# Batches of two block pairs in the attention stage of a two-layer hybrid encoder, with the PSUM banks divided anew

## The chip, the cores and the metric

The kernel runs on one core of a Trainium2 chip. The metric is the device time of one execution in microseconds (us). Times are medians of several executions; the profile is that of one more execution, with a time of its own.

## What is computed

A sequence of 2048 tokens with 1024 features passes two layers and a final norm. Layer 0 is a state-space scan and a convolution side by side. Layer 1 is attention over selected keys: a small indexer scores all admissible keys of a query, the 256 best are kept, and each of 16 query heads attends to them; four query heads share one key/value head. The part that the change touches, cut to what matters:

```python
def block(c):                      # 64 queries
    score = einsum("bqh,bqhs->bqs", wib, relu(einsum("bqhd,bsd->bqhs", qib, ki)))
    score = where(key_chunk <= c, score, -inf)
    _, idx = top_k(score, 256)
    logits = einsum("bqhgd,bqkhd->bqhgk", qb, k[idx]) * 64 ** -0.5
    p = softmax(where(valid, logits, -inf))
    return einsum("bqhgk,bqkhd->bqhgd", p, v[idx])
```

All of it is in float32. The kernel does not gather keys: it computes the scores of all admissible keys and adds a mask of 0 or -1e30.

## The kernel before

The program is traced in Python, and a scheduler then orders each engine's instructions by a model of their times, with earlier traced instructions first among those that are ready. An engine executes its list in order. `K.after(later, earlier)` adds an edge to that ordering between two instructions of one engine, without a semaphore.

Layer 0, the projections of layer 1 and the indexer come first, then the attention stage (class `Attend`), then the output projection (`layer1_out`). The attention stage goes through 16 row tiles of 128 queries, in the order `ORDER`; row tile i has nb = i+1 key blocks of 128 keys. Each row tile is done in two halves `kp` (two key/value heads, e = 0 and 1), each half in two units `hp`; a unit holds two query heads h for each e. So there are 64 units. Beside the attention, the selection of keys for row tiles 12 to 15 (`select_mask`, generator `beside`) runs on DVE, ACT and GpSimd; one step of it is traced for every `PACE` = 800 columns of scores.

For a unit, `weights` makes the scores: for each h and each half of up to 1024 keys, it takes two tiles of two PSUM banks (pool `pq`, one for each e), fills them by matmuls of at most 512 columns in two parts (high and low part of the keys, L1095), and reads each with one DVE instruction (L1099). This one scales, adds the mask, writes `lm` (tile `prob`) and keeps a running minimum `mx`, which the second half takes as its start value. One ACT instruction for each (h, e) then exponentiates the whole row (L1110).

`values` goes over groups (e, b): two key blocks of one e. Four transposes by TensorE (L1126: two blocks, two heads) fill one bank of pool `pt` (three banks, tag `pt`), ACT copies them to SBUF as `pT` (L1131; for more than 14 blocks every second group is copied by DVE, L1129), and two products with v (L1133) accumulate in the one bank of pool `pv`. A product fills 64 columns of the array; the two of a group write different halves of the partitions. Each product appears in the trace as two matmul records, each transpose as one. After the last group, ACT copies the sums (`ov`, L1137), TensorE transposes them (`ps_ot`, L1141) into the same bank, and DVE multiplies them by the gate and the inverse denominator (L1147, L1150).

The queries of the next half are transposed in `stacks` (`ps_q`, L772); these tiles also come from pool `pt`. In the main loop the scores of a unit are traced before the values of the unit before it:

```python
unit = (loaded[n], hp_, at.weights(loaded[n], hp_))
if hp_ == 0:
    ready(n + 1)
if pend:
    at.values(*pend)
pend = unit
```

`chunks(n)` already exists for the indexer: it cuts n columns into pieces of at most 512 within each 1024, and makes a piece 384 wide where 128 columns would be left over.

## Time and profile before

| | |
|---|---|
| median of 3 runs | 3005.96 us (3002.47 to 3012.47) |
| profiled execution | 3008.15 us |
| its span, first to last instruction | 3006.3 us |
| TensorE busy | 2754.0 us (92%) |
| DVE busy | 2127.9 us (71%) |
| ACT busy | 1694.8 us (56%) |
| GpSimd busy | 1118.3 us (37%) |
| mean granted TensorE clock | 0.969 |

Shares over the whole span are averages over stages. In a busy time, overlapping instructions of one engine count once; matmuls are pipelined, so TensorE can be busy all the time and still be slowed. What TensorE does is better read from the distances between the starts of its instructions in the timeline.

### The profile page before, as it was taken

What the parts mean: (1) busy time and instruction counts of PE and PEld (TensorE: products, weight loads), DVE (VectorE), ACT (ScalarE), POOL (GpSimd) and SP (SyncE); (2) the same over time, 40 slices, a digit from 0 to 9 for tenths busy, and PEclk for the clock granted to TensorE, in tenths of its full rate; (3) what the DMA queues carried; (4) which work ended last, traced back from release to release, by engine and by line L of the source; (5) the groups of instructions that cost most, each with busy time, mean ns of one, the idle gap of its engine ahead of it and who ended that gap; (6) DMA issues with size and microseconds to landing.
All of it is one profiled execution on the core that took longest, in us unless ns stands there. A gap on an engine that the chain in (4) does not pass through costs nothing.

```text
span 3006.3 us, 47629 instructions
## 1 busy us (share of the span) xinstructions
PE 2754.0 (92%) x17488; PEld 2223.8 (74%) x17488; DVE 2127.9 (71%) x4121; ACT 1694.8 (56%) x3202; POOL 1118.3 (37%) x1453
## 2 busy tenths in 40 slices
PE   7779998799999999899789898999989999999998
PEld 5657786677999898888778885666655666666787
DVE  8889895996354478979997877876777444456444
ACT  4122333334243688778856558888887767655311
POOL 3946132642231587765665323322322101001000
PEclk9889899899999999999899998999999999999999
DMA  3263554356557323223432424110110101001332
GB/s 135 72 131 127 161 158 81 114 168 194 183 186 249 100 71 109 77 84 104 140 109 77 128 92 162 38 57 29 61 38 28 49 18 43 22 5 50 123 126 98
DMA packets 233385, 300.40 MB, mean 100 GB/s; under 512 B 14144, under 2 KB 171072, under 8 KB 233024
## 3 DMA queue, kind: packets, MB, share of 16 engines
q1 hardware_dynamic: 233152, 297.37, 31.5%
q8 instruction: 137, 2.24, 0.3%
q14 instruction: 96, 0.79, 0.1%
HBM read 194.16 MB, written 105.25 MB: 100 GB/s over the span
## 4 chain that ended last, share of the span: by engine, by line
PE 41%; DVE 19%; issue 6%; ACT 5%; POOL 5%; DMA 3%; SPq 0%; DVEq 0%; ACTq 0%; POOLq 0%
PE ps_pv L1133 9%; PE ps_pt L1126 8%; PE ps_s L1095 7%; DVE eq L976 6%; PE ps_tm L121 2%; PE ps_tm L122 2%; PE ps_tm L123 2%; PE ps_o L122 2%; PE ps_o L121 2%; PE ps_o L123 2%; DVE scl L72 2%; POOL sv L69 2%; ACT eq L986 1%; DVE cum L1026 1%; POOL wl L114 1%
## 5 line engine op out<-in xcount | busy, mean ns | idle before, releaser
L114 POOL TENSOR_TENSOR wl<-wst,wh 128x512 fp32r<-128x512 f32 (+1 forms) x220 | 339.0, 1544 | 389.6 <-ACT wh L113 377.8
L121 PE MATMUL ps_tm<-wh,hb 128*128 128x256 f32 (+1 forms) x1536 | 439.4, 290 | 11.7 <-ACT ot L875 7.5
L122 PE MATMUL ps_tm<-wh,hb 128*128 128x256 f32 (+1 forms) x1536 | 444.1, 290 | 0.2 <-DVE hb L72 0.2
L123 PE MATMUL ps_tm<-wl,hb 128*128 128x256 f32 (+1 forms) x1536 | 438.8, 289 | 0.0
L1099 DVE CUSTOM_DVE_ANT_0 lm<-ps_s,amb 128x1024 f32<-128x1024 f32 (+7 forms) x256 | 250.3, 987 | 200.1 <-PE ps_pt L1126 117.2
L72 DVE SCALAR_TENSOR_TENSOR cvo<-hc,vec,cvo 128x1024 f32<-128x1024 f32 x240 | 359.3, 1529 | 0.8
L1131 ACT COPY pT<-ps_pt 128x512 f32<-128x512 f32 (+1 forms) x512 | 273.9, 564 | 152.3 <-PE ps_pt L1126 130.1
L1133 PE MATMUL ps_pv<-pT,v 128*64 128x256 f32 x2176 | 339.3, 398 | 14.4 <-DVE avt L62 7.5
L1126 PEld LDWEIGHTS ps_pt<-ident,lm 128*128 128x128 f32 x2176 | 240.1, 141 | 145.4 <-issue 124.5
L1126 PE MATMUL ps_pt<-ident,lm 128*128 128x128 f32 x2176 | 339.1, 282 | 6.1 <-ACT pT L1131 4.0
L1110 ACT ACTIVATE lm<-lm,mx 128x512 f32<-128x512 f32 (+15 forms) x256 | 309.1, 1211 | 62.9 <-DVE mx L1099 62.4
L69 POOL TENSOR_SCALAR sv<-sv 128x1 f32<-128x1 f32 x448 | 185.5, 415 | 382.6 <-DVE eq L976 296.5
L121 PEld LDWEIGHTS ps_tm<-wh,hb 128*128 128x128 f32 x1536 | 296.2, 194 | 21.2 <-ACT ot L875 9.2
L122 PEld LDWEIGHTS ps_tm<-wh,hb 128*128 128x128 f32 x1536 | 297.7, 194 | 6.0 <-DVE hb L72 0.6
L123 PEld LDWEIGHTS ps_tm<-wl,hb 128*128 128x128 f32 x1536 | 296.4, 194 | 4.8
L113 ACT CAST wh<-wst 128x512 fp32r<-128x512 f32 (+1 forms) x220 | 133.4, 610 | 277.2 <-DMA wst<-in_w_in 122.3
L1095 PE MATMUL ps_s<-kh,qs 128*128 128x512 f32 (+2 forms) x640 | 264.9, 415 | 19.4 <-DVE mx L1099 17.9
L121 PE MATMUL ps_p<-hh,wh 128*128 128x512 f32 x640 | 258.5, 406 | 19.1 <-ACT uT L520 16.0
L123 PE MATMUL ps_p<-hl,wh 128*128 128x512 f32 x640 | 258.9, 407 | 0.0
L122 PE MATMUL ps_p<-hh,wl 128*128 128x512 f32 x640 | 257.5, 403 | 0.0
L1095 PE MATMUL ps_s<-kl,qs 128*128 128x512 f32 (+2 forms) x640 | 233.4, 370 | 0.0
L913 ACT ACTIVATE relu<-ps_i 128x512 f32<-128x512 f32 (+3 forms) x304 | 161.0, 545 | 104.5 <-DVE scl L72 55.3
(327 smaller groups left out, 6353.0 us busy)
## 6 DMA issues: line engine op xcount, KB each, us to landing
wst<-in_w_in SPq DMA_DIRECT2D x168, 256.0 KB, 2.9
zs_d<-zt SPq DMA_DIRECT2D x16, 512.0 KB, 3.5
zt<-zs_d SPq DMA_DIRECT2D x16, 512.0 KB, 4.5
ry<-rec_d SPq DMA_DIRECT2D x16, 512.0 KB, 4.2
xr<-in_x SPq DMA_DIRECT2D x16, 512.0 KB, 4.3
wst<-in_w_out SPq DMA_DIRECT2D x32, 256.0 KB, 3.3
h_d<-xr SPq DMA_DIRECT2D x16, 512.0 KB, 3.5
xt<-h_d SPq DMA_DIRECT2D x16, 512.0 KB, 6.1
```

The source lines that it names most:

```text
L69: eng.tensor_scalar(out=out, in0=a, scalar1=s1, scalar2=s2, op0=op0, op1=op1)
L72: self.nc.vector.scalar_tensor_tensor(out=out, in0=a, scalar=s, in1=b, op0=op0, op1=op1)
L114: nc.gpsimd.tensor_tensor(out=lo, in0=st, in1=hi.bitcast(F32), op=ALU.subtract)
L121: t.matmul(ps, a[0], b[0], start=start, stop=False)
L122: t.matmul(ps, a[1], b[0], start=False, stop=False)
L123: t.matmul(ps, a[0], b[1], start=False, stop=stop)
L1095: nc.tensor.matmul(pss[e][:, cols], qs[e][:, 2 * hp + h], src[:, e, cols], start=part == 0, stop=part == 1)
L1099: self.pace[0] = nc.vector.tensor_tensor_reduce(out=prob[e][h][:, c:c + w], in0=pss[e][:, 0:w], in1=mb[:, c:c + w], scale=-0.125, scalar=( ...
L1110: nc.scalar.activation(lm, lm, AF.Exp, bias=mxs[e, h][:, nh - 1:nh], scale=-1.0, accum_out=t["den"][:, hd:hd + 1])
L1126: nc.tensor.transpose(ps[:, s, h], prob[e][h][:, (b + s) * P:(b + s + 1) * P], ident)
L1131: nc.scalar.copy(pT[:, 0:n], ps[:, 0:n].rearrange("p s h q -> p s (h q)"))
L1133: nc.tensor.matmul(po[64 * s:64 * s + 64, e], self.kvt[(b + s) // 8, kp][2][:, (b + s) % 8, e * 64:e * 64 + 64], pT[:, s], start=b == 0, s ...
```

## The change

1. `weights`: the scores of each h go over `chunks(nk)`, pieces of at most 512 columns. For each piece two one-bank tiles are taken (pool `pq`, now three banks in place of two tiles of two), filled by four matmuls and read by one DVE instruction each. The running minimum passes from piece to piece; `mx` has five columns.
2. `values`: groups are handled in batches of `TURN` = 2. `turned` makes the transposes and the copy of one group, `weighted` the products of a batch. The products of a batch are traced after the transposes of the next batch, and an edge ties the first of them behind the last of these transposes. Another edge (`held`) ties the first transpose of a call behind the last product of the call before.
3. Pool `pt2` has four banks in place of three. Eight PSUM banks are in use before and after.

```diff
--- before.py
+++ after.py
@@ -1041,7 +1041,7 @@
         self.k, self.S, self.kvt, self.ident, self.identr = k, S, kvt, ident, identr
         self.am, self.tm, self.qsp, self.ap, self.pp, self.ptp, self.pq, self.pt, self.pv_ = pools
         self.beside, self.pace, self.cols = beside, pace, 0
-        self.masks = {}
+        self.masks, self.held = {}, None
 
     def load(self, i, kp):
 
@@ -1072,7 +1072,7 @@
 
         k, nc, ap_, kvt = self.k, self.k.nc, self.ap, self.kvt
         nk = (t["i"] + 1) * P
-        kp, qs, mb, nh = t["kp"], t["qs"], t["mb"], (nk + HALF - 1) // HALF
+        kp, qs, mb, ch = t["kp"], t["qs"], t["mb"], chunks(nk)
         prob = [[None, None], [None, None]]
         mxs = {}
         for h in range(2):
@@ -1082,24 +1082,21 @@
                 elif h == 0:
                     both = self.pp[e].tile([P, 2, HALF], F32, tag="lm", name="lm")
                     prob[e] = [both[:, 0], both[:, 1]]
-                mxs[e, h] = ap_.tile([P, 2], F32, tag="mx", name="mx", bufs=8)
-            for half in range(nh):
-                c = half * HALF
-                w = min(HALF, nk - c)
-                kh, kl, _ = kvt[half, kp]
-                pss = [self.pq.tile([P, HALF], F32, tag="pq", name="ps_s") for _ in range(2)]
-                for b in range(0, w, 512):
-                    cols = slice(b, b + max(min(512, w - b), 256))
-                    for part, src in enumerate((kh, kl)):
-                        for e in range(2):
-                            nc.tensor.matmul(pss[e][:, cols], qs[e][:, 2 * hp + h], src[:, e, cols],
-                                             start=part == 0, stop=part == 1)
+                mxs[e, h] = ap_.tile([P, 5], F32, tag="mx", name="mx", bufs=8)
+            for ci, (c, w) in enumerate(ch):
+                pss = [self.pq.tile([P, 512], F32, tag="pq", name="ps_s") for _ in range(2)]
+                half, m = c // HALF, max(w, 256)
+                cols = slice(c % HALF, c % HALF + m)
+                for part in range(2):
+                    for e in range(2):
+                        nc.tensor.matmul(pss[e][:, 0:m], qs[e][:, 2 * hp + h], kvt[half, kp][part][:, e, cols],
+                                         start=part == 0, stop=part == 1)
                 for e in range(2):
                     mx = mxs[e, h]
                     self.pace[0] = nc.vector.tensor_tensor_reduce(
                         out=prob[e][h][:, c:c + w], in0=pss[e][:, 0:w], in1=mb[:, c:c + w], scale=-0.125,
-                        scalar=(-NEG if half == 0 else mx[:, 0:1]), op0=ALU.add, op1=ALU.min,
-                        accum_out=mx[:, half:half + 1])
+                        scalar=(-NEG if ci == 0 else mx[:, ci - 1:ci]), op0=ALU.add, op1=ALU.min,
+                        accum_out=mx[:, ci:ci + 1])
                     self.cols += 2 * w
                     while self.cols >= PACE:
                         self.cols -= PACE
@@ -1107,7 +1104,7 @@
             for e in range(2):
                 lm = prob[e][h][:, 0:nk]
                 hd = 4 * e + 2 * hp + h
-                nc.scalar.activation(lm, lm, AF.Exp, bias=mxs[e, h][:, nh - 1:nh], scale=-1.0,
+                nc.scalar.activation(lm, lm, AF.Exp, bias=mxs[e, h][:, len(ch) - 1:len(ch)], scale=-1.0,
                                      accum_out=t["den"][:, hd:hd + 1])
         return prob
 
@@ -1117,22 +1114,46 @@
         nb, kp = t["i"] + 1, t["kp"]
         np_ = P if nb > 1 else 64
         po = self.pv_.tile([P, 2, 256], F32, tag="pv", name="ps_pv")
-        for e in range(2):
-            for b in range(0, nb, 2):
-                n = min(2, nb - b)
-                ps = self.pt.tile([P, 2, 2, 128], F32, tag="pt", name="ps_pt")
+
+        def turned(group):
+
+            e, b = group
+            n = min(2, nb - b)
+            ps = self.pt.tile([P, 2, 2, 128], F32, tag="pt", name="ps_pt")
+            for s in range(n):
+                for h in range(2):
+                    op = nc.tensor.transpose(ps[:, s, h], prob[e][h][:, (b + s) * P:(b + s + 1) * P], ident)
+                    if self.held is not None:
+                        k.after(op, self.held)
+                        self.held = None
+            pT = self.ptp.tile([P, 2, 256], F32, tag="pT", name="pT")
+            if b % 4 == 2 and nb > 14:
+                nc.vector.tensor_copy(pT[:, 0:n], ps[:, 0:n].rearrange("p s h q -> p s (h q)"))
+            else:
+                nc.scalar.copy(pT[:, 0:n], ps[:, 0:n].rearrange("p s h q -> p s (h q)"))
+            return e, b, n, pT, op
+
+        def weighted(groups, last):
+
+            for e, b, n, pT, _ in groups:
                 for s in range(n):
-                    for h in range(2):
-                        nc.tensor.transpose(ps[:, s, h], prob[e][h][:, (b + s) * P:(b + s + 1) * P], ident)
-                pT = self.ptp.tile([P, 2, 256], F32, tag="pT", name="pT")
-                if b % 4 == 2 and nb > 14:
-                    nc.vector.tensor_copy(pT[:, 0:n], ps[:, 0:n].rearrange("p s h q -> p s (h q)"))
-                else:
-                    nc.scalar.copy(pT[:, 0:n], ps[:, 0:n].rearrange("p s h q -> p s (h q)"))
-                for s in range(n):
-                    nc.tensor.matmul(po[64 * s:64 * s + 64, e],
-                                     self.kvt[(b + s) // 8, kp][2][:, (b + s) % 8, e * 64:e * 64 + 64], pT[:, s],
-                                     start=b == 0, stop=b + s >= nb - 2)
+                    op = nc.tensor.matmul(
+                        po[64 * s:64 * s + 64, e],
+                        self.kvt[(b + s) // 8, kp][2][:, (b + s) % 8, e * 64:e * 64 + 64], pT[:, s],
+                        start=b == 0, stop=b + s >= nb - 2)
+                    if last is not None:
+                        k.after(op, last)
+                        last = None
+            self.held = op
+
+        groups = [(e, b) for e in range(2) for b in range(0, nb, 2)]
+        before = None
+        for g in range(0, len(groups), TURN):
+            now = [turned(group) for group in groups[g:g + TURN]]
+            if before:
+                weighted(before, now[-1][4])
+            before = now
+        weighted(before, None)
         ov = ap_.tile([P, 2, 256], F32, tag="ov", name="ov", bufs=2)
         nc.scalar.copy(ov[0:np_], po[0:np_])
         ps = self.pv_.tile([P, 2, 2, 128], F32, tag="pv", name="ps_ot")
@@ -1156,6 +1177,7 @@
 ORDER = (3, 7, 4, 6, 5, 8, 2, 9, 1, 10, 11, 12, 0, 13, 14, 15)
 RATIO = 2
 CHAINS = 3
+TURN = 2
 EARLY = 140
 PACE = 800
 LATE = 12
@@ -1275,8 +1297,8 @@
             am, tm = pool(c3, "am", 1, side="right"), pool(c3, "tm", 1, side="right")
             ptp, ap_ = pool(c3, "ptp", 4, side="right"), pool(c3, "ap", 1, side="right")
             pp1, qsp = pool(c3, "pp1", 3, side="right"), pool(c3, "qsp", 1, side="right")
-            pools = (am, tm, qsp, ap_, (pp0, pp1), ptp, pool(c3, "pq", 2, space=PSUM),
-                     pool(c3, "pt2", 3, space=PSUM), pool(c3, "pv", 1, space=PSUM))
+            pools = (am, tm, qsp, ap_, (pp0, pp1), ptp, pool(c3, "pq", 3, space=PSUM),
+                     pool(c3, "pt2", 4, space=PSUM), pool(c3, "pv", 1, space=PSUM))
             at = Attend(k, S, kvt, pools, ident, identr, beside, pace)
             halves = [(i, kp) for i in ORDER for kp in range(2)]
             loaded = {}
```

## Rows read from the trace of the kernel before

**Rows 1.** Busy times by stretch: from:to, length, each engine (instructions), clock, DMA

```profile
1815.00:2310.00 495.00, 455.92 (x2946) 308.92 (x2945) 369.29 (x799) 422.88 (x771) 136.20 (x255) 0.98 0.16 53
2310.00:2809.00 499.00, 496.47 (x3232) 325.52 (x3230) 255.28 (x502) 312.62 (x494) 65.31 (x90) 1.00 0.10 32
```

**Rows 2.** Waits of weight loads, 1815 to 2310 us: total us, times, longest

```profile
PEld ps_pt L1126 <- issue: 49.8, 129, 0.8
PEld ps_s L1095 <- DVE mx L1099: 29.5, 42, 2.5
...
PEld ps_pv L1133 <- ACT pT L1131: 13.6, 35, 2.2
```

**Rows 3.** The same view, 2310 to 2809 us

```profile
PEld ps_pt L1126 <- issue: 74.7, 194, 0.4
```

**Rows 4.** Timeline of TensorE, groups one by one: start us, length us, instruction, count

```profile
2403.84 0.66 PE L1126 MATMUL ps_pt<-ident,lm 128*128 128x128 f32 x4
2404.42 0.65 PE L1133 MATMUL ps_pv<-pT,v 128*64 128x256 f32 x4
2405.01 0.66 PE L1126 MATMUL ps_pt<-ident,lm 128*128 128x128 f32 x4
```

**Rows 5.** Timeline of TensorE, a place where two groups went together

```profile
2649.72 1.09 PE L1126 MATMUL ps_pt<-ident,lm 128*128 128x128 f32 x8
2650.74 1.08 PE L1133 MATMUL ps_pv<-pT,v 128*64 128x256 f32 x8
2651.75 0.66 PE L1126 MATMUL ps_pt<-ident,lm 128*128 128x128 f32 x4
```

**Rows 6.** Timeline of TensorE, first and last run of value products

```profile
1827.42 0.65 PE L1133 MATMUL ps_pv<-pT,v 128*64 128x256 f32 x4
...
2806.97 1.52 PE L1133 MATMUL ps_pv<-pT,v 128*64 128x256 f32 x12
```

**Rows 7.** Timeline of TensorE, query transposes between value products

```profile
2308.40 0.65 PE L1133 MATMUL ps_pv<-pT,v 128*64 128x256 f32 x4
2308.98 0.53 PE L772 MATMUL ps_q<-identr,tmq 128*128 128x128 f32 x4
2309.45 0.65 PE L1133 MATMUL ps_pv<-pT,v 128*64 128x256 f32 x4
```

**Rows 8.** Timeline of TensorE, scores between transposes and value products

```profile
2406.18 0.66 PE L1126 MATMUL ps_pt<-ident,lm 128*128 128x128 f32 x4
2406.59 0.48 PE L1095 MATMUL ps_s<-kh,qs 128*128 128x512 f32 x1
...
2407.47 0.65 PE L1133 MATMUL ps_pv<-pT,v 128*64 128x256 f32 x4
```

**Rows 9.** Timeline of TensorE, score pieces of 384 and 512 columns

```profile
2639.88 0.34 PE L1095 MATMUL ps_s<-kl,qs 128*128 128x384 f32 x1
2640.05 0.39 PE L1095 MATMUL ps_s<-kh,qs 128*128 128x512 f32 x1
2640.28 0.40 PE L1095 MATMUL ps_s<-kl,qs 128*128 128x512 f32 x1
```

**Rows 10.** DVE by line and shape, 1815 to 2810 us: busy us, mean ns, idle before

```profile
L1099 DVE CUSTOM_DVE_ANT_0 lm<-ps_s,amb 128x1024 f32<-128x1024 f32 x144 | 175.5, 1221 | 149.3 <-PE ps_pt L1126 92.1 <-PE ps_s L1095 56.6
...
L1099 DVE DVE_READ_ACCUMULATOR2_ANT mx<- 128x1 f32 x384 | 31.9, 83 | 0.0
...
L1099 DVE CUSTOM_DVE_ANT_0 lm<-ps_s,amb,mx 128x512 f32<-128x512 f32 x16 | 11.9, 749 | 11.1 <-PE ps_s L1095 11.0
...
L1099 DVE CUSTOM_DVE_ANT_0 lm<-ps_s,amb 128x512 f32<-128x512 f32 x16 | 10.7, 688 | 3.4 <-PE ps_s L1095 3.2
```

**Rows 11.** By stretch, instructions that write or read `lm`: PE, PEld, DVE, ACT

```profile
1815.00:2310.00 495.00, 154.99 (x996) 110.88 (x996) 169.34 (x207) 168.84 (x318) 0.98 0.16 53
```

**Rows 12.** ACT by line, 1815 to 2810 us: busy us, mean ns, idle before

```profile
L1110 ACT ACTIVATE lm<-lm,mx 128x512 f32<-128x512 f32 (+15 forms) x256 | 309.1, 1211 | 62.9 <-DVE mx L1099 62.4
L1131 ACT COPY pT<-ps_pt 128x512 f32<-128x512 f32 (+1 forms) x512 | 273.9, 564 | 152.3 <-PE ps_pt L1126 130.1 <-PE ps_pv L1133 20.8
```

## The prediction

> **What bounds the kernel now.** I read the table of time stretches first. The change touches only the attention stage, which runs from about 1815 to 2809 us of a span of 3006.3 us; I cut it at 2310 us, shortly before the selection of keys that runs beside it ends. In the second part TensorE is busy for 496 of 499 us, and DVE for only 255 and ACT for 313 [rows 1]. In the first part TensorE is busy for 456 of 495 us, ACT for 423 and DVE for 369 [rows 1]: three engines are close to each other there, and TensorE waits for them. So a saving on TensorE shortens the second part in full and the first part only partly. What follows the stage starts when its rows are done, so I pass a shorter stage on to the end in full.
>
> Next the waits. In the first part TensorE's weight loads stand still 29.5 us for a minimum from DVE (a score bank not yet read) and 13.6 us for ACT's copy of transposed weights [rows 2]. In both parts the largest entry has no releaser at all: before a transpose that follows a value product, 129 and 194 times, some 0.39 us each [rows 2, 3]. The timeline shows what that is. Call T the four transposes of one group (two key blocks) and W its two value products (four records). Where T and W alternate, T at 2403.84, W at 2404.42, T at 2405.01, one round takes 1.17 us [rows 4]. Where two groups went together, T8 at 2649.72, W8 at 2650.74, T4 at 2651.75, two groups took 2.03 us [rows 5]. Two rounds would be 2.34 us, so each round saved is worth 0.31 us: TensorE pays at each turn between the full-width transposes and the products that fill half of its columns.
>
> Counted along the timeline, from the first value product at 1827.42 to the last at 2806.97 [rows 6], the 576 groups are executed in 406 unbroken runs of value products: 175 for 242 groups in the first part, 231 for 302 in the second (the rest lies at the cut and in records missing from the trace). Turns thus cost about 406 x 0.31 = 126 of the 994 us.
>
> **The change part by part.** *Fewer turns.* Every call of `values` has an even number of groups, so two make a batch: 288 batches. The edges written out give T T, then W of the batch before, and the next call's transposes come after the last W, so the last two batches of a call share one run. With nothing else in between, a call of n batches has n-1 runs (one if n=1). That is 104 runs in the first part and 127 in the second.
>
> Two things break runs. Queries' transposes use the same banks as T and cut runs now: W at 2308.40, query transposes at 2308.98, W at 2309.45 [rows 7]; only these stand between two runs in 20 places of the first part and 15 of the second. I keep all of them. Scores are traced before the values and enter wherever a bank falls free. Between T and W they cost no further turn (T at 2406.18, scores at 2406.59, W at 2407.47 [rows 8]), between two W they do. Now that is 13 and 9 places. A batch of four products offers three inner places instead of one, and a score bank frees once per 512 columns, not per 1024, so up to twice as often. Threefold would be 39 and 27, sixfold 78 and 54. I take 25 and 35, since in the second part the batches are longer; the first part's share is near its old value because its runs are shorter. Runs afterwards: 104+20+25 = 149 and 127+15+35 = 177. Saved: 26 and 54, together 80 x 0.31 = -24.8 us. The ends are none (0 us) and all (406-231 = 175 runs, -54 us).
>
> *Score pieces.* For 5 and 13 key blocks the old cut leaves 512 and 256 columns computed, the new one 384 and 256. A piece of 512 takes 0.23 us (2640.05 to 2640.28), one of 384 takes 0.17 (2639.88 to 2640.05) [rows 9]. 32 matmuls in each of the two row tiles save 0.06: -3.8 us. The rest of the score columns stays.
>
> *More reduces on DVE.* Pieces go from 24 to 40 over the 16 row tiles, times 16: 384 reduces become 640. Splitting 1024 columns replaces 1221+83 ns by 688+83 and 749+83 ns [rows 10]: 299 ns each, 256 x 0.299 = 76.5 us of DVE. 112 of them, 33.5 us, belong to the ten row tiles of the first part, 43 us to the second. In the second part the cover is DVE's idle 244 us, so I cost it at nothing there. In the first, DVE would be busy 403 of 495 us. TensorE waits 29.5 us there for 169 us of reduces [rows 11], 0.17 us per us; at that rate 33.5 us more cost +6 us. Ends: 0, and 33.5 if DVE passes everything on. Two things speak for the lower half: the third bank lets the next piece of one head begin before the other's is read, and a 0.7 us reduce blocks DVE's queue for less time than a 1.2 us one. Behind each reduce on DVE are queued the next piece's reduce, the selection's counts and, for 15 and 16 key blocks, half of the weights' copies.
>
> The Trainium skill has a rule that speaks against this part (VectorE: DVE Perf Modes, on the trn2 errata): a fixed cost per DVE instruction, measured there as about 150 cycles at 0.96 GHz, so that many small pieces pay it each. Worked out from that page it is an estimate of 256 x 0.156 = 40 us, 17.5 of it early. The rows show 299 ns for a split and not 156, because the second piece takes its start value from a column and each piece has an accumulator read of its own [rows 10]; I use 299.
>
> *A longer way from T to W.* W now follows the next batch's T, so a copy by ACT (564 ns on average [rows 12]) has a T8 and the W8 before it, 2.03 us, to finish, against one round of 1.17. That takes away part of the first part's 13.6 us: -7, between -13.6 and 0. Four T banks hold two batches, and four `pT` buffers do too, since W of a batch is issued before the T that needs its buffers again.
>
> *The ends of the calls.* The last W has only the W of the batch before to cover its copies, 1.0 us for two copies in sequence, and the next call's transposes may not come first. ACT is in an exponential for 309 of 994 us, 1.2 us at a time [rows 12]. If one is in the way (one call in three) W waits about 0.8 us unless scores fill it: 64/3 x 0.8 = 17 us at most; the 8 calls of one batch have no cover, about 1.2 us each or 10 us. Scores of the next unit stand before values in priority and should fill most. I take +6, between 0 and 27; nearer to 0, as calls now end T, W with one group's cover and the second part shows hardly a wait.
>
> Sum: -24.8 -3.8 +6 -7 +6 = -23.6 us. The profiled execution took 3008.15 us (span 3006.3); 3008.15-23.6 = 2984.5. It lies 2.2 us above the median of 3005.96, so the forecast for the median is 2982.
>
> **The rivals.** *Scores cut the batches up.* Every bank that falls free starts its own pair of score matmuls, up to 640 entries. If 80 more than I took fall inside a run of W, the turns stay at 406. Left are -3.8+6-7+6 = +1: 3007, no change. For it: entries get shorter and more frequent. Against: of some 300 entries now only 22 stand alone between two runs.
>
> *The first part becomes DVE's* (the slower side). All 33.5 us of the additional reduces reach TensorE through the score banks, the relief of 7 us disappears in it, and the call ends cost 6: -24.8-3.8+33.5+6 = +11, 3017. It becomes slower than can be told from no change (0.3%, 9 us) when additional waits exceed 24.8+3.8+9 = 37.6 us. For it: DVE at 369 of 495 us and 29.5 us of waits on it already; against: ACT is busier there, and DVE also waits for TensorE's scores.
>
> *Clean batches.* No score and no query cuts a run (231 runs, -54), pieces -3.8, all 13.6 us of the copies' waits go and nothing is added: -71, 2935; with the query cuts left and half of the waits, -54+11-3.8-7 = -54, 2952.
>
> *The edges don't hold.* Each binds one instruction only. If the others pass it, the order remains near the old one, with the pieces and the reduces changed: about -3.8+6, 3008.
>
> **How the numbers follow.** Forecast 0.47 (2970 to 2997), cut-up batches 0.20, DVE 0.14, clean batches 0.14, edges 0.05. Faster by over 0.3%: nearly all of the first, the clean batches and a little of the cut-up ones, 0.62; within 0.3%: 0.22; slower: the DVE case and a tail of the others, 0.16. The range goes from the moderate clean case, 2950, to the DVE case, 3017; beyond lie half of the clean and half of the DVE chance.
>
> **What would show it.** Runs of value products near 326, most of eight records, and fewer than 323 entries "transpose, no releaser". In the second part of the stage TensorE still without waits and some 18 us shorter. 640 reduces at about 690 to 750 ns. In the first part, the wait of scores for DVE: under 40 us for the forecast, over 60 for the DVE rival. The wait of value products for ACT's copy: less than 13.6 us in the first part; if it grows, the call ends were priced too low. I am wrong in the main step if runs stay near 400, and wrong in the sum if runs fall and a wait on DVE or ACT takes their place.

## The result, and the profile after

| | before | after |
|---|---|---|
| median, beside each other | 3004.22 us (4 executions) | 3034.28 us (4; 3023.94 to 3041.96) |
| ratio, 95% interval | 1 | 1.0092 [1.0065, 1.0118] |
| profiled execution | 3008.15 us | 3023.94 us |
| its span | 3006.3 us | 3022.2 us |
| attention stage, first score to last value product | 1814.6 to 2808.1 | 1808.2 to 2819.8 |
| first part, to the end of the tenth row tile | 518.6 us | 548.5 us |
| second part | 475.5 us | 463.6 us |
| unbroken runs of value products, by part | 184 + 222 | 171 + 192 |
| mean granted TensorE clock | 0.969 | 0.966 |

The kernel became slower by about 0.9%, where 0.8% faster was forecast. A second measurement of the same kernel gave 1.0084 [1.007, 1.0098] (e14 below). The four executions of the first took 3023.94, 3030.53, 3038.03 and 3041.96 us at mean clocks of 0.966, 0.964, 0.962 and 0.960, and the profile is of the fastest; it shows half of the loss in the medians. The stretch ahead of the stage was 6.4 us shorter in it. That stretch has the same order of TensorE's instructions in both kernels, so I take its 6.4 us as scatter from execution to execution. The stage grew by 18.1 us, all in the first part. In the profile of e14, the same kernel at about its median (3031.05 us), the stage is 23.6 us longer than before. One execution of e1 below ran in a slower state of the chip (3113.51 us at a clock of 0.837); its median counts it, its ratio doesn't. From here on the parts are cut at the end of the tenth row tile, not at 2310 us, so that both kernels have the same work in them.

Busy times of the kernel after, by stretch (columns as in [rows 1]; PE, PEld, DVE, ACT, POOL, clock, DMA):

```profile
1808.00:2357.00 549.00, 490.98 (x3097) 330.96 (x3098) 410.81 (x1068) 439.90 (x802) 138.20 (x262) 0.95 0.15 53
2357.00:2820.00 463.00, 458.88 (x3057) 303.61 (x3055) 251.60 (x744) 292.12 (x464) 59.32 (x84) 1.00 0.09 29
```

TensorE fills the second part as before. In the first part it stands for 58 us, against 40 before with the same cut, and its clock is 0.95, against 0.98 in [rows 1].

Waits of weight loads in the kernel after, first part, then second (line, releaser, total us, times, longest):

```profile
PEld ps_s L1092 <- DVE mx L1096: 56.2, 70, 5.0
PEld ps_pt L1125 <- issue: 39.2, 96, 0.8
PEld ps_pv L1140 <- issue: 37.5, 105, 2.8
PEld ps_pv L1140 <- ACT pT L1133: 11.5, 30, 2.3
```

```profile
PEld ps_pt L1125 <- issue: 48.9, 127, 0.4
PEld ps_pv L1140 <- ACT pT L1133: 15.8, 47, 1.3
```

Against [rows 2], the wait of scores for DVE has nearly doubled, from 29.5 us (31.2 with the parts cut as here) to 56.2, and its longest has gone from 2.5 to 5.0 us. The entry "transpose, no releaser" fell as forecast, from 129 and 194 to 96 and 127 times. Beside it stands "value product, no releaser". It was there before too, 73 and 156 times, in lines that [rows 2] and [rows 3] leave out (1815 to 2310 us, then 2310 to 2809):

```profile
PEld ps_pv L1133 <- issue: 17.4, 73, 1.5
```

```profile
PEld ps_pv L1133 <- issue: 30.6, 156, 0.4
```

After, these are 105 times and 37.5 us in the first part, 96 times and 23.1 us in the second. So in the first part some of what was saved before transposes is paid again before products.

Here is one of the long waits, in the timeline of DVE and TensorE (some other instructions left out):

```profile
2248.97 2.35 DVE L976 TENSOR_SCALAR_CACHE_REDUCE eq<-khi,sv 128x2048 bf16<-128x2048 uint16 x1
...
2249.32 0.33 PE L1092 MATMUL ps_s<-kl,qs 128*128 128x384 f32 x1
...
2251.24 2.35 DVE L72 SCALAR_TENSOR_TENSOR klo<-khi,sv,klo 128x2048 uint16<-128x2048 uint16 x1
...
2253.57 0.68 DVE L1096 CUSTOM_DVE_ANT_0 lm<-ps_s,amb 128x512 f32<-128x512 f32 x1
...
2254.31 0.69 PE L1092 MATMUL ps_s<-kh,qs 128*128 128x384 f32 x1 [4.66 <-DVE mx L1096]
```

The scores of a piece are in their bank at about 2249, but two instructions of the selection (a count, L976, and an update of `klo`, L72) are ahead of the reduce in DVE's queue. The next score matmul needs that bank and stands 4.66 us at the head of TensorE's queue; all that is behind it, transposes and products too, stands with it. During the waits of scores in the first part such selection instructions ran on DVE for 4.3 us before and for 25.5 us after.

What follows the wait costs again. Busy times around it, and TensorE's timeline there:

```profile
2243.00:2249.00 6.00, 5.84 (x40) 4.13 (x40) 5.83 (x17) 4.79 (x8) 1.90 (x5) 1.00 0.12 44
2249.00:2254.00 5.00, 0.66 (x5) 0.34 (x3) 5.00 (x5) 0.91 (x2) 1.99 (x4) 1.00 0.18 52
2254.00:2259.00 5.00, 4.69 (x19) 3.11 (x20) 3.31 (x15) 3.92 (x6) 1.29 (x2) 0.50 0.19 60
```

```profile
2255.25 1.98 PE L1140 MATMUL ps_pv<-pT,v 128*64 128x256 f32 x8
2257.16 1.97 PE L1125 MATMUL ps_pt<-ident,lm 128*128 128x128 f32 x8
```

TensorE was busy for 0.66 of 5 us, and in the next 5 us its granted clock is 0.50, the lower level of 1.2 GHz. Eight products take 1.98 us and eight transposes 1.97, against 1.08 and 1.09 in [rows 5]. In the first part, distances within runs of products or transposes that are about double occur 8 times before and 70 times after; what they cost beyond the single distance is 1.4 and 11.2 us.

**The account.** I took every distance between two starts on TensorE in the stage, subtracted the steady distance of that kind of matmul, and counted a rest over 150 ns as a wait and a shorter one as turn. Doubled distances of products and transposes are taken out of both and stand by themselves; score matmuls at the lower clock are left among the waits and turns.

| after minus before, profiled executions | us |
|---|---|
| stretch ahead of the stage | -6.4 |
| waits | +25.4 |
| products and transposes at the lower clock | +9.8 |
| turns | -9.5 |
| score pieces of 384 columns | -3.8 |
| rest of TensorE's work, mainly the output projection not yet begun in the stage | -3.9 |
| last value product to the end | +4.2 |
| sum (span: +15.9) | +15.8 |

The turns themselves did what was forecast: the rests from product to transpose and from transpose to product fell from 55.9 to 34.8 us. The scores gave it back in short rests, 31.1 to 41.5 us between score matmuls, 13.4 to 22.2 from a score to a product and 3.5 to 9.3 from a product to a score. All other rests together fell by 13.4 us, about half of that between two transposes.

The last two lines above the sum belong together: they are work that moved. Before, the output projection's first matmul comes 18 us ahead of the last run of value products, and 24 of its matmuls (some 5.5 us) lie inside the stage; after, it begins behind the last product:

```profile
2788.94 0.48 PE L121 MATMUL ps_o<-wo,yh 128*128 128x512 f32 x1
```

```profile
2818.21 1.95 PE L1140 MATMUL ps_pv<-pT,v 128*64 128x256 f32 x16
2820.08 0.50 PE L121 MATMUL ps_o<-wo,yh 128*128 128x512 f32 x1
```

The first fence is of the kernel before (its last run of products is in [rows 6]), the second of the one after. TensorE is full in both cases, so little is lost or gained by it. Of the 12 us by which the second part is shorter, some 5 are therefore no gain.

**One statement ahead of this is wrong.** The section on the change, and the prediction with it, say that the `held` edge ties a call's first transpose behind the last product of the call before. In the code every `weighted` sets `self.held`, within a call too. So the first transpose of every further batch is tied behind the last product before it, and together with the other edge this gives a strict alternation: transposes of a batch, products of the batch before, transposes of the next. The order may not place transposes ahead of a product that will wait.

### The profile page after: what moved, and what is told of

It reads as the page before. It is cut to its first block, busy times and chain, and to the rows that moved or that the text cites. A ratio compares the mean times of both kernels' runs of the same rounds, so it can differ in the third digit from the quotient of the medians.

```text
span 3022.2 us, 48310 instructions
## 1 busy us (share of the span) xinstructions
PE 2751.4 (91%) x17488; PEld 2223.9 (74%) x17488; DVE 2167.6 (72%) x4633; ACT 1691.0 (56%) x3202; POOL 1110.3 (37%) x1453
## 4 chain that ended last, share of the span: by engine, by line
PE 42%; DVE 18%; issue 6%; POOL 5%; ACT 4%; DMA 3%; SPq 0%; DVEq 0%; ACTq 0%; POOLq 0%
PE ps_pv L1140 10%; PE ps_pt L1125 8%; PE ps_s L1092 8%; DVE eq L976 6%; PE ps_tm L121 2%; PE ps_tm L122 2%; PE ps_tm L123 2%; PE ps_o L122 2%; PE ps_o L121 2%; PE ps_o L123 2%; POOL sv L69 2%; DVE scl L72 2%; ACT eq L986 1%; DVE lm L1096 1%; POOL wl L114 1%
## 5 line engine op out<-in xcount | busy, mean ns | idle before, releaser
L72 DVE SCALAR_TENSOR_TENSOR cvo<-hc,vec,cvo 128x1024 f32<-128x1024 f32 x240 | 357.3, 1520 | 0.8
L1096 DVE CUSTOM_DVE_ANT_0 lm<-ps_s,amb,mx 128x512 f32<-128x512 f32 (+3 forms) x384 | 244.1, 652 | 138.6 <-PE ps_s L1092 134.0
L1107 ACT ACTIVATE lm<-lm,mx 128x512 f32<-128x512 f32 (+15 forms) x256 | 307.9, 1208 | 55.8 <-DVE mx L1096 55.3
L1133 ACT COPY pT<-ps_pt 128x512 f32<-128x512 f32 (+1 forms) x512 | 263.6, 567 | 132.4 <-PE ps_pt L1125 131.4
L1125 PE MATMUL ps_pt<-ident,lm 128*128 128x128 f32 x2176 | 312.1, 282 | 1.3 <-ACT qs L774 0.8
L1092 PE MATMUL ps_s<-kh,qs 128*128 128x512 f32 (+2 forms) x640 | 273.0, 431 | 37.0 <-DVE mx L1096 35.1
L1096 DVE CUSTOM_DVE_ANT_0 lm<-ps_s,amb 128x512 f32<-128x512 f32 (+3 forms) x256 | 157.0, 629 | 119.4 <-PE ps_pt L1125 78.0
L1140 PEld LDWEIGHTS ps_pv<-pT,v 128*64 128x64 f32 x2176 | 138.8, 139 | 137.7 <-issue 60.6
```

The source lines that it names most:

```text
L72: self.nc.vector.scalar_tensor_tensor(out=out, in0=a, scalar=s, in1=b, op0=op0, op1=op1)
L1092: nc.tensor.matmul(pss[e][:, 0:m], qs[e][:, 2 * hp + h], kvt[half, kp][part][:, e, cols], start=part == 0, stop=part == 1)
L1096: self.pace[0] = nc.vector.tensor_tensor_reduce(out=prob[e][h][:, c:c + w], in0=pss[e][:, 0:w], in1=mb[:, c:c + w], scale=-0.125, scalar=( ...
L1107: nc.scalar.activation(lm, lm, AF.Exp, bias=mxs[e, h][:, len(ch) - 1:len(ch)], scale=-1.0, accum_out=t["den"][:, hd:hd + 1])
L1125: op = nc.tensor.transpose(ps[:, s, h], prob[e][h][:, (b + s) * P:(b + s + 1) * P], ident)
L1133: nc.scalar.copy(pT[:, 0:n], ps[:, 0:n].rearrange("p s h q -> p s (h q)"))
```

## The experiments

All ratios are against the kernel before, measured beside it on the same chip. "Waits" are those of the account, doubled distances of products included, first and second part; "slow" is the surplus of products and transposes at doubled distances in the first part.

| kernel | median us | ratio, 95% interval | runs of products | waits us | slow us |
|---|---|---|---|---|---|
| before | | 1 | 184 + 222 | 55.5 / 1.7 | 1.4 |
| after | 3034.28 | 1.0092 [1.0065, 1.0118] | 171 + 192 | 83.0 / 5.0 | 11.2 |
| e1 scores only | 3023.18 | 1.0046 [1.0029, 1.0063] | 174 + 269 | 59.3 / 3.2 | 4.9 |
| e2 batches only | 3003.81 | 0.9986 [0.9975, 0.9997] | 158 + 174 | 65.5 / 5.1 | 6.4 |
| e3 scores, four banks | 3016.23 | 1.0036 [1.0023, 1.0049] | 187 + 231 | 65.3 / 1.1 | 8.3 |
| e4 products first | 3027.81 | 1.0076 [1.0056, 1.0095] | 171 + 190 | 85.1 / 5.0 | |
| e5 before, selection traced early | 3013.18 | 1.0020 [1.0008, 1.0031] | 189 + 219 | 60.9 / 1.0 | |
| e6 after, selection traced early | 3004.98 | 0.9992 [0.9981, 1.0003] | 172 + 190 | 61.6 / 4.9 | 7.0 |
| e7 after, pace 1300 | 3021.77 | 1.0042 [1.0025, 1.0059] | 165 + 193 | 52.8 / 32.1 | |
| e8 batches, pace 1300 | 3008.86 | 0.9999 [0.9985, 1.0013] | 157 + 175 | 55.4 / 20.0 | |
| e9 before, no selection | 2926.0 | 0.9737 [0.9724, 0.9750] | 178 + 224 | 6.2 / 0.3 | 0.1 |
| e10 after, no selection | 2925.19 | 0.9734 [0.9709, 0.9759] | 154 + 191 | 10.9 / 5.0 | 1.2 |
| e11 after, banks 4 and 3 | 3010.36 | 1.0014 [1.0001, 1.0027] | 174 + 195 | 67.2 / 2.0 | 7.2 |
| e12 batches, selection traced early | 3017.78 | 1.0044 [1.0031, 1.0056] | 164 + 174 | 76.5 / 5.1 | 10.1 |
| e13 after, banks 3 and 3 | 3015.3 | 1.0034 [1.0021, 1.0047] | 171 + 197 | 67.3 / 4.5 | 8.4 |
| e14 after again | 3031.05 | 1.0084 [1.0070, 1.0098] | 171 + 192 | 86.5 / 5.0 | 15.3 |
| e15 batches late, edge left | 3346.41 | 1.1130 [1.1109, 1.1152] | 280 + 174 | 348.0 / 5.1 | |
| e16 batches late | 2998.07 | 0.9977 [0.9965, 0.9990] | 184 + 174 | 55.3 / 5.8 | 1.7 |
| e17 batches, no `held` | 2985.52 | 0.9929 [0.9912, 0.9946] | 158 + 165 | 59.1 / 2.0 | 4.1 |
| e18 after, no `held` | 3020.39 | 1.0048 [1.0034, 1.0063] | 174 + 267 | 59.6 / 3.2 | 5.3 |

### The two halves of the change: e1, e2, e3

e1 is the new `weights` and the new banks with the old `values`. e2 is the new `values` with both edges, with the old `weights` and banks. e3 is e1 with

```diff
-pool(c3, "pq", 3, space=PSUM), pool(c3, "pt2", 4, space=PSUM)
+pool(c3, "pq", 4, space=PSUM), pool(c3, "pt2", 3, space=PSUM)
```

> Only the scores' part of the change (pieces of 512, three score banks, four banks for transposes); the value products go group by group as before. In the changed kernel the matmuls of the scores wait 51 us for DVE's minimum in the first part of the stage (1808 to 2333 us), 29.5 us before. Theory REDUCES (256 more reduces on DVE, 299 ns each, 33.5 us of them beside the selection): the whole loss is here and the gain of the batches is missing, so 3030 to 3045 us, ratio 1.009 to 1.014. Theory BANKS (1536 instead of 2048 columns of scores can wait in PSUM while DVE is in a 2.3 us count of the selection): the same, 3030 to 3045. Theory BATCHES (the loss comes from the order of transposes and products and its edges): no loss, 2995 to 3010.

> Only the batches: transposes and products in batches of two groups with both edges, scores in two tiles of two banks as before, so three banks for transposes. Theories REDUCES and BANKS: runs of value products fall from 406 to 260 to 320, 0.31 us each, and no new wait for DVE: 2965 to 2990 us, ratio 0.988 to 0.996. Theory BATCHES: slower than before, 3010 to 3030.

> The scores' part with four banks of 512 columns for the scores, as many columns as before, and three banks for transposes; products group by group. The 640 reduces stay. Theory REDUCES: the loss stays, 3025 to 3040 us, ratio 1.007 to 1.012, and the wait of the scores for DVE in the first part stays near 50 us. Theory BANKS: no loss, 2995 to 3010, that wait near 30 us.

The scores alone cost 0.46%, and mainly in a place where I hadn't expected it: with the old groups the runs in the second part rise from 222 to 269 and that part from 475.5 to 486.0 us. The waits of scores rise by 8 us (27.5 to 35.5), near the +6 of the forecast; during them selection instructions ran on DVE for some 18 us in e1 too, against 4.3 before. The batches alone come to 332 runs, nearly the forecast number, and yet gain only 0.14%: the second part is 10.5 us shorter, the first 6.3 longer, its waits 10 us more. A fourth score bank (e3, 1.0036) doesn't take the loss away; its interval overlaps that of e1, so no effect of the banks on the time of the scores alone is shown. Neither half has the loss of the whole: +0.46% and -0.14% don't add up to +0.9%.

### Is it the order, or the selection beside it: e4 to e8, e12

e4 raises the scheduler's priority of the products by 1500 places; e5, e6 and e12 trace the whole selection ahead of the stage; e7 and e8 stretch it.

```diff
+            with k.tc.high_priority(offset=1500):   # e4, around the products
-EARLY = 140
+EARLY = 2000                                        # e5 (before), e6 (after), e12 (e2)
-PACE = 800
+PACE = 1300                                         # e7 (after), e8 (e2)
```

> The changed kernel, value products ahead of the scores in the order's priority, so that scores don't cut a batch. If the cuts (90 places with nothing but scores between two runs of products, 363 runs in all) are what ate the gain: runs fall under 290 and the time by 73 x 0.31 = 23 us, 3000 to 3015 us. If the loss is the wait of the scores for DVE in the first part: the runs fall as well, but the time by less than 10 us, above 3020, as scores come later and their reduces too.

> The kernel before, with all steps of the selection for row tiles 12 to 15 traced ahead of the attention stage (EARLY 2000 instead of 140), so that no selection stands on DVE and ACT beside the scores. It is the partner of the next run. Both theories: the first part of the stage gets shorter, what lies ahead of it longer; 3010 to 3080 us in all.

> The changed kernel with the selection ahead of the stage, as in the run before it. Theory SELECTION (the loss of 30 us in the first part comes from scores that wait behind selection instructions of 2 to 4 us on DVE; 25 us of such waits in the changed kernel, 4 before): without them only the gain of fewer turns is left, so this run is 5 to 20 us FASTER than the one with the old attention, in the first part too. Theory REDUCES (the 256 more reduces cost their 299 ns whatever stands beside): still slower by 10 us or more.

> The changed kernel with one selection step per 1300 columns of scores instead of 800: the selection is spread over more of the stage, into the part where DVE is idle for half of the time. Theory SELECTION: the scores' wait for DVE in the first part falls from 47 us to 25 to 35, the time to 3000 to 3015 us. Theory REDUCES: within 6 us of the changed kernel (3022 to 3034).

> Batches only (scores in two tiles of two banks, three banks for transposes) with one selection step per 1300 columns. The batches alone measured 0.9986 of the kernel before, with 10.5 us gained in the second part and 6 us lost to waits in the first. Theory SELECTION: these waits shrink, 2980 to 2995 us, ratio 0.992 to 0.997. If the waits have another cause: 2998 to 3006 us.

> Batches with the old scores (two tiles of two banks, 384 reduces), the selection's steps traced ahead of the stage and so without the edges that tie each of its counts behind a reduce. With the changed scores this way of tracing took 61.6 us of waits in place of 83 in the first part. If the edges on the counts are what sets the waits there, 2985 to 2998 us, below every run so far; if the selection as such does, near 3004, the batches' own time.

e4 hardly changed the order (88 places with scores alone between two runs, against 90), so it says nothing of either theory.

e5, e6 and e12 did not do what their edit says: earlier tracing didn't take the selection out of the stage. It still has 200 us on DVE there and only ends sooner, at 2278 in place of 2333 us; what changed is where the scheduler places its instructions, and that its counts are no longer tied to the reduces. With that the loss of the kernel after is gone (0.9992, waits 61.6), that of the kernel before rises (1.0020), and the batches alone lose 0.44%, where I had expected a gain. Against its partner e5, e6 is 8 us faster, as the selection theory forecast; but e12 moved the other way under the same edit. I read this as the outcome hanging on which long instructions happen to stand ahead of which reduces; that is argued and not shown, and e6 is no evidence of a cure.

e7 and e8 show that the waits go where the selection goes. Both times missed what the selection theory forecast (3000 to 3015 and 2980 to 2995 us): spreading the selection moved the waits and didn't remove them. At PACE 1300 it ends at 2623 us, and the second part, which hardly waited before, then waits as well. Waits of weight loads in e7, 2322 to 2820 us:

```profile
PEld ps_s L1092 <- DVE mx L1096: 31.8, 53, 2.4
```

The sum of waits is nearly the same as in the kernel after (84.9 against 88.0 us), spread over both parts, and the two profiled spans, 3020.0 and 3022.2 us, are as near to each other. By the medians e7 is 0.4% slower than before and the kernel after 0.9%, but the profile of the kernel after is of its fastest execution.

### The selection left out: e9, e10

```diff
-                    yield from select_mask(k, j, sc, tk, L, 1, S["mask"], pace)
+                    all_mask(k, j, tk, L, S["mask"])
```

> The kernel before without the selection for row tiles 12 to 15: their mask is set to the plain causal one, so 200 us of DVE and 107 us of ACT disappear from the attention stage. It is the partner of the next run. 2940 to 2985 us under each theory.

> The changed kernel without the selection for row tiles 12 to 15, as in the run before it. Theory SELECTION (the loss is scores that wait behind long selection instructions on DVE): with none of them beside, the change gains what its fewer turns give, 406 to 363 runs at 0.31 us and 3.8 us of score pieces, so 10 to 20 us FASTER than the partner. Theory REDUCES (the 256 reduces of 299 ns as such): still 5 to 30 us slower than the partner.

The mask of row tiles 12 to 15 is then the plain causal one, and the selection is gone from ACT and GpSimd as well as from DVE. Waits of scores for DVE, 1800 to 2360 us, in e9 and then in e10:

```profile
PEld ps_s L1095 <- DVE mx L1099: 2.5, 6, 0.8
```

```profile
PEld ps_s L1092 <- DVE mx L1096: 11.1, 33, 0.4
```

Without the selection the change costs nothing: 0.9734 against 0.9737. The 256 additional reduces are all there, with 33 waits and none over 0.4 us. So the reduces alone don't make the loss; the selection beside them is needed for it. That it acts through DVE's queue is read from the long waits in the trace above, not from this pair. The sum of DVE's work is not the whole cause either: e11, e13 and e18 have the same 640 reduces and the same selection as the kernel after, and wait for 59.6 to 67.3 us in the first part instead of 83.0. In e10 hardly anything is gained, with 57 runs fewer: both first parts take 464 us, and the second goes from 466.2 to 461.5. The profiles have this gain of 4.6 us in the stage, and a stretch ahead of it, the same order of TensorE's instructions in both, that was 5.5 us longer.

### The banks: e11, e13, e14

e11 is the kernel after with four score banks and three for transposes. e13 has three of each and leaves one bank unused. e14 is the kernel after, unchanged.

```diff
-pool(c3, "pq", 3, space=PSUM), pool(c3, "pt2", 4, space=PSUM)
+pool(c3, "pq", 4, space=PSUM), pool(c3, "pt2", 3, space=PSUM)   # e11
+pool(c3, "pq", 3, space=PSUM), pool(c3, "pt2", 3, space=PSUM)   # e13
```

> The changed kernel with four banks for scores and three for transposes; reduces, pieces and batches stay. Theory BANKS (1536 columns of scores in PSUM are too few to bridge a selection instruction of 2.3 us on DVE, 2048 were enough): the first part's waits fall from 83 to under 65 us, the time to 2995 to 3012 us. If the number of banks doesn't matter: 3020 to 3035 us and waits of 75 us or more.

> The changed kernel with three banks for the scores and three for the transposes, one PSUM bank unused. It differs from the kernel with four and three (ratio 1.0014, waits of 67 us in the first part) by one score bank alone. Theory BANKS (scores can't bridge a selection instruction with three banks): the loss stays, 3018 to 3035 us, 78 us of waits or more in the first part. If that kernel was better by the chance of another order: 3005 to 3015 us, waits under 72. The free bank also tells of the hand-over: if the next stage's first output matmuls need a bank that neither scores nor transposes hold, they run ahead of the last value product again (24 of them, as before), and what follows that product takes 198 us, not 202.

> The changed kernel once more, on the same chip as the two beside it, to compare with them and to see how far its waits differ from execution to execution. Ratio 1.005 to 1.012; waits of 75 to 95 us in the first part, 202 us behind the last value product.

Waits of scores for DVE, 1800 to 2360 us, in e11, e13 and e14:

```profile
PEld ps_s L1092 <- DVE mx L1096: 35.0, 50, 4.1
```

```profile
PEld ps_s L1092 <- DVE mx L1096: 42.8, 60, 4.4
```

```profile
PEld ps_s L1092 <- DVE mx L1096: 56.8, 71, 5.0
```

A fourth score bank, at the cost of one for transposes, brings 35.0 us in place of 56 and a time only 0.14% above that of the kernel before. If the number of score banks were the whole cause, e13 would have kept the loss; it kept 0.34% of the 0.84% that e14 lost beside it. With three of each the waits are 67 us and the ratio is 1.0034. So it is the combination of three score banks and four transposes' banks that is worst. e14 shows that it is no accident of one measurement.

The expectation that e13 would begin the output projection early also failed: it begins behind the last product (2806.49 us, last run of products at 2804.61), as in all kernels with three score banks, while in e11 it is at 2794.99, 18 us ahead of the last product. Why the number of score banks decides that I have only argued (the bank that the projection gets first), not shown.

### Where the batches pay, and what the edge costs: e15 to e18

e15 makes batches from the eleventh row tile on only, but each single group still sets `held`. e16 is the same without that. e17 and e18 drop one line of e2 and of the kernel after.

```diff
+        if t["i"] in ORDER[:10]:          # e15, e16
+            for group in groups:
+                weighted([turned(group)], None)
+                self.held = None          # e16 only
+            groups = []
...
-            self.held = op                # e17 (from e2), e18 (from after)
```

> Batches only, and only in the six row tiles from the eleventh on, where no selection stands beside; the ten row tiles before go group by group, scores as before. If the batches' gain of some 10 us in the second part and their loss of some 6 us in the first are both the order's doing: 2990 to 2999 us, ratio 0.995 to 0.9975. If the two parts hang together (a gain behind is lost to a later start): 3000 to 3006 us.

> As the run with batches from the eleventh row tile on, but without the edge that there remained between single groups: in that run it tied each group's transposes behind the products of the group before, in the ten row tiles that were to go as before, which cost 348 us of waits (3346 us). Here those ten go group by group with no edge. If the batches' gain in the second part (10 us) stands by itself: 2990 to 2999 us, ratio 0.995 to 0.9975, first part within 5 us of the kernel before's 519. If it is given back elsewhere: 3000 to 3008 us.

> Batches only (two score tiles of two banks, three transposes' banks), without the edge that holds a call's first transposes behind the last products of the call before. The prediction gave that edge 6 us. If it costs that much: ratio 0.9955 to 0.9975 where the batches with it measured 0.9986, waits of the first part near 58 us instead of 65.5. If it costs nothing: 0.998 to 1.000.

> The changed kernel without the edge that holds a call's first transposes behind the last products of the call before; pieces, batches and banks stay. Without it the batches alone went from 0.9986 to 0.9929 of the kernel before (17 us). If the edge costs the changed kernel as much: ratio 1.001 to 1.005, waits of the first part between 60 and 75 us. If it is the cause of the first part's additional waits there: under 1.000, waits under 60. If three score banks beside four transposes' banks are the cause, with or without the edge: 1.006 to 1.010, waits of 78 us or more.

e15 was to leave the first part as before and made it 67% longer, through an edge that I had not seen. It is the clearest measurement of that edge. Waits and timeline in e15:

```profile
PEld ps_pv L1143 <- ACT pT L1136: 223.0, 208, 3.3
```

```profile
2003.28 0.65 PE L1128 MATMUL ps_pt<-ident,lm 128*128 128x128 f32 x4
...
2005.90 0.65 PE L1143 MATMUL ps_pv<-pT,v 128*64 128x256 f32 x4 [1.14 <-ACT pT L1136]
```

With a batch of one the edge allows no transposes in advance; each product waits for the copy of its own group, 208 times and 223 us. Without it (e16) the first part is as before (518.9 us), and the second, with batches, is 7.4 us shorter. There turn time falls from 71.7 to 60.3 us for 48 runs less: 0.24 us for each.

e17 is the batches without the new scores and with only the products tied; the tie at the ends of the calls is gone too. It has 158 + 165 = 323 runs, where 326 were forecast for the whole change, no more waits in the second part than before, and takes 2985.52 us (2981.43 to 2990.68), faster than both kernels. Its stage by stretch, cut at its own tenth row tile:

```profile
1814.00:2329.00 515.00, 473.36 (x3076) 327.23 (x3077) 390.88 (x827) 434.35 (x796) 137.55 (x262) 0.98 0.16 53
2329.00:2789.00 460.00, 458.80 (x3101) 319.75 (x3101) 235.39 (x474) 297.61 (x472) 61.08 (x85) 1.00 0.10 33
```

Against e2 the edge costs 16 us in the profiled executions (spans of 3002.4 and 2986.5) and 18 in the medians: waits are 6.4 us more with it in the first part (slow products included) and 3.1 in the second, and there are 9 more runs. How much of this is the tie within the calls and how much the one between them is not separated: the one line makes both.

In e18 dropping the same line lowers the waits too (83.0 to 59.6), but the batches fall apart, and the second part has 267 runs. Timeline of e18:

```profile
2614.77 0.65 PE L1140 MATMUL ps_pv<-pT,v 128*64 128x256 f32 x4
2615.35 0.33 PE L1125 MATMUL ps_pt<-ident,lm 128*128 128x128 f32 x1
2615.61 0.65 PE L1140 MATMUL ps_pv<-pT,v 128*64 128x256 f32 x4
```

A single transpose slips in between the two groups of products; nothing forbids it any more, and it costs two turns. The banks have a part in that: e1 and e3, alike but for them, have 269 and 231 runs in the second part, and e17, with three for transposes and the old scores, has 165. So with three score banks and four for transposes the edge is needed to have batches at all, and with the edge come the waits.

## Why the prediction was wrong, step by step

- **What bounds the kernel**: right. The second part is TensorE's, the first is shared, and the loss lies in the first. I had seen 29.5 us of waits for DVE [rows 2] and didn't ask what DVE does in them. The timeline of before would have shown a few waits behind selection instructions of up to 2.35 us (4.3 us in all); I priced the reduces as if DVE's queue held reduces.
- **Fewer turns, -24.8**: the mechanism held, the term was mis-sized in both factors. Saved were 43 runs, not 80, and some 0.22 us each (-9.5), not 0.31. Of the 363 runs 151 have eight records and 150 have four, where most of eight was expected. Scores alone stand between two runs of products in 90 places (41 and 49), where I took 60, and were 22 before; both lie within my threefold and sixfold bounds. The price came from places without scores [rows 4, 5]; more and shorter score matmuls between the runs brought short rests of their own, 25 us against the 21 saved between transposes and products. In e16, with the old scores, a run saved was worth 0.24 us. In e17 the count came to 323, near the forecast, but not by the forecast's parts: scores alone stand in 32 places there, not 60, and 127 of its runs have four records. That agreement is luck. (Without breaks the second part has 128 runs, not 127, which changes nothing.)
- **Score pieces, -3.8, and 299 ns for a split reduce**: right. DVE by line and form in the kernel after:

```profile
L1096 DVE CUSTOM_DVE_ANT_0 lm<-ps_s,amb,mx 128x512 f32<-128x512 f32 x224 | 163.2, 746 | 83.4 <-PE ps_s L1092 80.7
L1096 DVE CUSTOM_DVE_ANT_0 lm<-ps_s,amb 128x512 f32<-128x512 f32 x192 | 129.7, 687 | 87.3 <-PE ps_pt L1125 57.9 <-PE ps_s L1092 28.3
...
L1096 DVE DVE_READ_ACCUMULATOR2_ANT mx<- 128x1 f32 x640 | 53.1, 83 | 0.0
```

  687 + 83 + 746 + 83 - 1304 ns is 295, against the 299 from [rows 10]. The fixed cost alone that the Trainium skill states (VectorE: DVE Perf Modes, on the trn2 errata), about 150 cycles or by estimate 156 ns, would have been half of it; the trace decides for 295.
- **What the reduces do to TensorE, +6**: right for the scores alone (+8 in e1 and e18), wrong for the whole. The failed step is the cost put on DVE's queue: "the third bank lets the next piece of one head begin before the other's is read, and a 0.7 us reduce blocks DVE's queue for less time than a 1.2 us one". In the long waits what blocks the queue is not a reduce but one or two selection instructions of 2.35 us, and a small bank that is not read stops all of TensorE just as a large one does. The waits of the stage grew by 25.4 us, where this term and the next two together gave +5. By the wait for DVE the prediction's own test came out between its marks, 56.2 us where under 40 was for the forecast and over 60 for the DVE rival.
- **A longer way from T to W, -7**: 13.6 became 11.5 us in the first part, and the second has 15.8 us of such waits where there were 4.2 before. In sum not a gain but a loss; by the distances, all waits of the second part grew from 1.7 to 5.0 us.
- **The ends of the calls, +6**: built on the misreading of `held`. The edge acts on every batch, not once per call. Both kinds of tie together cost 16 to 18 us with the old scores. In the kernel after, the waits of the first part are 83.0 us with them and 59.6 without (e18). That they leave fewer transposes to be placed ahead of a late score is my reading of it, not shown.
- **The clock**: not in the sum at all. 9.8 us more of products and transposes at the lower level. By the clock records of the traces, 16.6 us of the stage were at that level before and 53.3 us after. The timeline of before had such places too: 8 doubled distances.
- **The sum**: from -23.6 to the profile's +15.8 us, the turns account for 15.3 us, the waits for 20.4, the clock for 9.8, and the shorter stretch ahead of the stage for -6.4.
- **The rivals**: "the first part becomes DVE's" had the right side, at 3017 against 3034, and +25 us of waits where it took 33.5, but its mechanism, the additional reduces' time passed on through the banks, is not supported: the same reduces are harmless in e10 and cost 8 us in e1. "Scores cut the batches up" was true for half of its mechanism, with runs at 363. "The edges don't hold" was wrong; they held too well.

What stays open: why three score banks with four transposes' banks and the edge wait for 83 us where three and three wait for 67. In e13 the transposes can't run a fourth bank ahead and in the kernel after they can, but by which planned order that puts more selection instructions ahead of the reduces (25.5 us against 16.2) I haven't found. Nor are the opposite signs of e5, e6 and e12 explained. Taking the selection off DVE, with all of it computed, wasn't tried, nor the new scores with four banks and without `held`, nor the tie between calls without the one within them.

## What to carry to other kernels

Before making a tile smaller, look at what else is in the queue of the engine that empties it: an in-order engine with 2.35 us instructions of another job sets the wait, not the instruction that you cut in two. An edge that forces an order has a price wherever the forced instruction can be late, so count how often it is set (each batch or each call), and try the kernel without it first: here one line was worth some 17 us with the old scores. When two edits trade the same resource, PSUM banks here, measure each by itself; neither of these two showed the loss that they have together.

## What the runs showed of the hardware

- After 5 us in which TensorE was busy for 0.66 us its granted clock was 0.50 for the next 5 us, and products and transposes took nearly twice their time (1.98 us for 1.08, 1.97 for 1.09). In the first part the lower level cost products and transposes 11.2 us in the kernel after, 15.3 in its second measurement, 7.2 in e11, 4.1 in e17, 1.4 before and 0.1 in e9. So in this kernel a long wait cost more than itself, and many short ones hardly did (e10: 33 waits of scores up to 0.4 us, 1.2 us at the lower clock).
- A turn between full-width transposes and half-width products is worth 0.31 us where nothing stands between, and 0.24 us on average over 48 turns saved in the whole of a part.
